# Trunk of two layers, float32: a weight sum of the MLP's seven-product scheme made by GpSimd instead of VectorE

## The chip, the cores and the metric

The program runs on 1 core of one Trainium2 chip. The metric is the device time of one execution in microseconds (us). The engines are TensorE (PE in the profile), VectorE (DVE), ScalarE (ACT), GpSimd (POOL) and SyncE (SP). The work of each engine is a queue in a fixed order; semaphores hold an instruction until its inputs are there.

## What is computed

The input `x` is 256 rows of 2048 numbers. Layer 1 is attention with forget gates, then an MLP; layer 2 is attention over chunks with a shared K/V, then an MLP. All weights are float32. The change lies in the two MLPs and in the query projection of layer 2, each a large matrix product:

```python
def sq_relu_mlp(h, g, w1, w2):            # w1: 2048 x 8192, w2: 8192 x 2048
    a = jax.nn.relu(rms_norm(h, g) @ w1)
    return (a * a) @ w2
...
q = rms_norm((u @ b_w_q[l]).reshape(B, S, H, Dh), b_q_g[l])   # b_w_q: 2048 x 2048
```

## The kernel before

**Splitting.** Each float32 product is made of three TensorE passes. Weights arrive in tiles of 128 x 1024. For each, ScalarE rounds it into `hi` (line 292), VectorE makes `lo = weight - hi` (line 293), and TensorE multiplies activations by `hi`, the activations' low part by `hi`, and the activations by `lo` (lines 592, 594, 596). Three pairs of `hi` and `lo` exist, so that the splits can run at most about two tiles ahead of TensorE.

**Seven products in place of eight.** In the MLPs and the query projection, half of the depth is done by blocks: a 2 x 2 block product takes seven products, with sums of weight blocks as operands. The class `Pair` holds one such set. Its seven weight operands are called f0 to f6, in two halves s = 0, 1 of 128 x 1024 each, and they come from four weight blocks 11, 12, 21, 22:

```python
FORMS = ("11", "T3", "T2", "T1", "21", "T4", "22")
```

T3 is 12 + 22, added in memory by a DMA that GpSimd issues (`add_on`, line 324); T2 is T3 + 11, added by an engine into a tile of its own, `wT2` (`make`, line 331); T1 is 11 + 12, again such a DMA, onto the tile of 11 once f0 has been split and T2 has been made; T4 is T2 + 21, added by VectorE in place (line 322). `bring` (line 311) loads 11 and 12 by SP. The profile cuts the numbers from names: `wT` is `wT2`, and `w` is `w11` or `w12`.

**Pairs.** There are 34: for each MLP, four chunks with two pairs of the up-projection (`w10`, `w11`) and two of the down-projection (`w20`, `w21`), and two pairs (`q0`, `q1`) of the query projection. With two halves that makes 68 additions at line 331. The table `ORDER` writes the order of each kind of pair out by hand; `f` is a seven-product operand, `a` and `b` are plain weight tiles of the same pair, `r` those left over from the pair before:

```python
"w10": "f0 f1 r f2 r r f4 f3 r r f5 a f6 a a a b b",
"w11": "f0 r f1 r f2 f4 a r f3 r a a f5 a f6 b b",
"w20": "r f0 r r f1 f2 f4 f3 f5 a r r a r b f6 b",
"w21": "f0 f1 f2 r f3 f4 r a f5 r r f6 r b a r",
```

**Where T2 is made.** `issue` splits an operand, and `behind` then runs what the table `BEHIND` lists for it. `(0, 1, "make", 0)` stands at f0, so that `make` comes right behind the split of f0 of the same half. It reads the tiles of T3 and of 11 and writes `wT2`, whose last readers were the splits of f5 (T4) of the pair before.

**Other work.** GpSimd issues the accumulating DMAs of line 324, half of the small DMAs that turn activations (`moves`, line 456), and a few powers of 128 x 4 (line 691). VectorE also makes the activations' low parts (lines 421, 965), transposes (441), sums of activations (399 to 402), and the corrections of the seven products (637, 639). `keep_order` fixes the written order on VectorE, ScalarE, TensorE and SyncE; on GpSimd the scheduler sets it.

Of the kernel before, what the change touches and what calls it, by code (L numbers as in the profile page):

```python
# [12 lines left out]
ALU = mybir.AluOpType  # L13
# [85 lines left out]
def trunk(ctx: ExitStack, tc: tile.TileContext, t):  # L99
# [3 lines left out]
    V, S, G, TE, SY = nc.vector, nc.scalar, nc.gpsimd, nc.tensor, nc.sync  # L103
# [200 lines left out]
    def half(s):  # L304
        return slice(s * UN, (s + 1) * UN)
# [20 lines left out]
    def make(p, s):  # L326
        assert (not p.prev or p.prev.did(5)) and {("T3", s), ("11", s)} <= p.done
        p.done.add(("T2", s))
        if not s:
            p.t["T2"] = qkv.tile([P, BIG], F32, name="wT2", tag="Z", bufs=1)  # L330
        V.tensor_tensor(p.t["T2"][:, half(s)], p.t["T3"][:, half(s)], p.t["11"][:, half(s)], op=ALU.add)  # L331

    later = deque()

    def behind(p, i, s):
        for k in range(s, 2 if s == p.subs - 1 else s + 1):
            for d, own, f, *a in BEHIND.get((i, k), ()):
                q = p if own else p.next
                if q is not None and a[-1] < q.subs:
                    while len(later) < d + 1:  # L340
                        later.append([])
                    later[d].append(lambda f=f, q=q, a=a: WAYS[f](q, *a))

    WAYS = {"make": make, "add": add_on, "bring": bring}

    def fetch(ahead=AHEAD, early=EARLY):
# [82 lines left out]
    def steps(make):  # L429
        box = []  # L430

        def step():
            if not box:
                box.append(make())
            next(box[0])
        return step
# [706 lines left out]
```

## Time and profile before

| | before |
|---|---|
| median of 2 runs | 2119.57 us (2119.49 to 2119.66) |
| the profiled execution | 2115.48 us, its span 2113.7 us |
| TensorE busy | 2074.7 us, 98% of the span |
| VectorE busy | 1736.8 us, 82% |
| ScalarE busy | 1301.9 us, 62% |
| GpSimd busy | 354.1 us, 17% |
| granted TensorE clock | 0.998 |

The span runs from the first to the last instruction; the execution's own time is 1.8 us longer. A row of a group gives the source line, the engine, what is written from what, the shape and count, and then busy time and the mean of one in ns; behind the second bar it gives the idle time of the engine just before these instructions. A row of the timeline gives start and length in us, then the instruction, and in square brackets the idle time before it and what ended it; "x2" is two such instructions that follow each other, and their length is that of both.

### The profile page before, as it was taken

The page shows a single profiled execution, that of the slowest core. Times are in us where ns is not written, and L with a number is a line of the kernel's source. Part 1 is how long each engine was busy: PE and PEld are TensorE (multiplying, and loading weights), DVE is VectorE, ACT ScalarE, POOL GpSimd, SP SyncE. Part 2 cuts the span into 40 slices and gives each one's busy share as a digit, 9 for nine tenths or more (in the row PEclk, how much of TensorE's full clock was granted, in tenths as well). Part 3 has the DMA queues.
Part 4 walks back from the last instruction along what each step waited for, and adds up shares of the span by engine and source line. Part 5 has one row for each costly group of instructions (what it writes and reads, how often), then busy time and mean ns, then how long its engine had stood idle before and what let it go on. Part 6 is the DMA issues. An engine that isn't in the chain of part 4 may idle for free.

```text
span 2113.7 us, 27078 instructions
## 1 busy us (share of the span) xinstructions
PE 2074.7 (98%) x9114; PEld 1695.1 (80%) x9114; DVE 1736.8 (82%) x2003; ACT 1301.9 (62%) x1567; POOL 354.1 (17%) x552
## 2 busy tenths in 40 slices
PE   9999999999999999999999999999999999999999
PEld 7888888787887887887777888887878878878877
DVE  6777776998889889878989577768988998898897
ACT  6544445676567567557767445456765765675674
POOL 1101002221031022022224000022200310220220
PEclk9999999999999999999999999999999999999999
DMA  8777788889888888898786777888897898888884
GB/s 302 241 257 222 240 253 266 251 257 283 273 256 245 277 267 244 262 278 268 239 241 218 256 235 241 239 265 251 268 278 256 259 259 279 268 250 256 280 262 157
DMA packets 160636, 538.89 MB, mean 255 GB/s; under 512 B 42849, under 2 KB 68081, under 8 KB 125681
## 3 DMA queue, kind: packets, MB, share of 16 engines
q1 hardware_dynamic: 129136, 453.78, 61.3%
q0 software_dynamic: 31360, 83.39, 20.8%
q8 instruction: 71, 1.16, 0.2%
q14 instruction: 69, 0.56, 0.1%
HBM read 497.20 MB, written 15.75 MB: 243 GB/s over the span
## 4 chain that ended last, share of the span: by engine, by line
PE 83%; DMA 6%; DVE 6%; issue 3%; ACT 2%; SPq 0%; POOL 0%; ACTq 0%; DVEq 0%; POOLq 0%
PE acc L592 18%; PE acc L594 18%; PE acc L596 18%; PE po L592 5%; PE po L596 5%; PE po L594 5%; PE s L596 4%; PE s L592 4%; PE s L594 4%; DVE lo L293 3%; DMA raw<-in_s2a 2%; DMA q<-z 2%; ACT hi L292 2%; DVE wT L322 1%; DMA raw<-in_s2b 1%
## 5 line engine op out<-in xcount | busy, mean ns | idle before, releaser
L293 DVE TENSOR_TENSOR lo<-raw,hi 128x1024 fp32r<-128x1024 f32 (+1 forms) x634 | 759.5, 1214 | 221.2 <-ACT hi L292 208.9
L292 ACT ACTIVATE hi<-raw 128x1024 fp32r<-128x1024 f32 (+1 forms) x634 | 660.4, 1054 | 386.7 <-PE acc L594 224.5
L592 PE MATMUL acc<-hi,act 128*128 128x512 f32 x1644 | 459.0, 394 | 9.9 <-DVE acc L637 4.4
L596 PE MATMUL acc<-lo,act 128*128 128x512 f32 x1644 | 449.1, 390 | 0.3 <-DVE lo L293 0.3
L594 PE MATMUL acc<-hi,act 128*128 128x512 f32 x1644 | 449.1, 390 | 0.0
L592 PEld LDWEIGHTS acc<-hi,act 128*128 128x128 f32 x1644 | 306.1, 188 | 79.5 <-DVE acc L637 7.9
L596 PEld LDWEIGHTS acc<-lo,act 128*128 128x128 f32 x1644 | 307.5, 188 | 66.8 <-DVE lo L293 2.4
L594 PEld LDWEIGHTS acc<-hi,act 128*128 128x128 f32 x1644 | 308.5, 188 | 65.5 <-DVE act L387 0.5
L292 ACT ACTIVATE hi<-w 128x1024 fp32r<-128x1024 f32 x204 | 215.1, 1056 | 100.6 <-PE acc L594 39.6
L293 DVE TENSOR_TENSOR lo<-w,hi 128x1024 fp32r<-128x1024 f32 x204 | 244.5, 1216 | 27.9 <-ACT hi L292 27.2
L456 POOL DMA_DIRECT2D q<-z x336 | 174.1, 608 | 464.1 <-DVE z L441 253.8
L292 ACT ACTIVATE hi<-wT 128x1024 fp32r<-128x1024 f32 x136 | 142.4, 1057 | 65.7 <-PE acc L594 27.0
L293 DVE TENSOR_TENSOR lo<-wT,hi 128x1024 fp32r<-128x1024 f32 x136 | 162.7, 1218 | 21.9 <-ACT hi L292 21.8
L596 PE MATMUL s<-lo,act 128*128 128x512 f32 x476 | 137.7, 394 | 2.6 <-DVE lo L293 2.4
L592 PE MATMUL s<-hi,act 128*128 128x512 f32 x476 | 136.4, 391 | 0.8 <-ACT hi L292 0.8
L594 PE MATMUL s<-hi,act 128*128 128x512 f32 x476 | 135.5, 389 | 0.0
L596 PEld LDWEIGHTS s<-lo,act 128*128 128x128 f32 x476 | 87.9, 188 | 27.0 <-DVE lo L293 9.7
L592 PEld LDWEIGHTS s<-hi,act 128*128 128x128 f32 x476 | 89.4, 188 | 20.6 <-ACT hi L292 2.0
L594 PEld LDWEIGHTS s<-hi,act 128*128 128x128 f32 x476 | 89.5, 188 | 18.8
L691 POOL TENSOR_TENSOR rn<-vv,mhalf 128x4 f32<-128x4 f32 x32 | 44.3, 1398 | 336.4 <-DVE vv L690 336.3
L331 DVE TENSOR_TENSOR wT<-w,w 128x1024 f32<-128x1024 f32 x68 | 82.7, 1217 | 0.0
L322 DVE TENSOR_TENSOR wT<-wT,raw 128x1024 f32<-128x1024 f32 x68 | 82.7, 1216 | 0.0
(183 smaller groups left out, 2282.1 us busy)
## 6 DMA issues: line engine op xcount, KB each, us to landing
raw<-in_w_in SPq DMA_DIRECT2D x94, 512.0 KB, 5.5
raw<-in_s1a SPq DMA_DIRECT2D x32, 1024.0 KB, 6.4
raw<-in_s2a SPq DMA_DIRECT2D x32, 1024.0 KB, 6.9
raw<-in_w_kv SPq DMA_DIRECT2D x64, 512.0 KB, 5.5
raw<-in_s1b SPq DMA_DIRECT2D x32, 1024.0 KB, 7.0
raw<-in_s2b SPq DMA_DIRECT2D x32, 1024.0 KB, 6.7
raw<-in_w_oa SPq DMA_DIRECT2D x32, 512.0 KB, 6.3
w<-in_f1a SPq DMA_DIRECT2D x16, 1024.0 KB, 7.0
```

Of the source, the lines that this page charges most:

```text
L292: S.activation(hi[:, c], raw[:, c], AF.Copy)
L293: V.tensor_tensor(lo[:, c], raw[:, c], hi[:, c].bitcast(F32), op=ALU.subtract)
L322: V.tensor_tensor(d, d, p.t["21", s], op=ALU.add)
L331: V.tensor_tensor(p.t["T2"][:, half(s)], p.t["T3"][:, half(s)], p.t["11"][:, half(s)], op=ALU.add)
L456: (SY, G)[j % 2].dma_start(d[32 * j : 32 * j + 32, i], z[32 * i : 32 * i + 32, j * n : (j + 1) * n])
L592: TE.matmul(ps, xh, cut(hi, j), start=first, stop=False, **kw)
L594: TE.matmul(ps, xl, cut(hi, j), start=False, stop=False, **kw)
L596: TE.matmul(ps, xh, cut(lo, j), start=False, stop=last, **kw)
L691: G.tensor_tensor(rn, vv, mhalf, op=ALU.pow)
```

## The change

The addition of T2 is issued on GpSimd's queue (`G` is `nc.gpsimd`, `V` is `nc.vector`). The place in the source is the same.

```diff
     def make(p, s):
         assert (not p.prev or p.prev.did(5)) and {("T3", s), ("11", s)} <= p.done
         p.done.add(("T2", s))
         if not s:
             p.t["T2"] = qkv.tile([P, BIG], F32, name="wT2", tag="Z", bufs=1)
-        V.tensor_tensor(p.t["T2"][:, half(s)], p.t["T3"][:, half(s)], p.t["11"][:, half(s)], op=ALU.add)
+        G.tensor_tensor(p.t["T2"][:, half(s)], p.t["T3"][:, half(s)], p.t["11"][:, half(s)], op=ALU.add)
```

On GpSimd, at the first `w20` and `w21` pair of layer 1 (`w11_3995` and `w11_4328` are their tiles of 11, `q` rows are the turning DMAs, `in_f2a0` and `in_f2a1` the weights), the queue now reads, with + for rows that are new:

```order
 L324 DMA w12_3808<-in_f2a0 128x1024 x2
 L456 DMA q_3836<-z_3835 32x256 x8
+L331 TENSOR_TENSOR wT2_4096<-w12_3808,w11_3995 128x1024 x2
 L456 DMA q_4034<-z_4033 32x256 x8
 L324 DMA w11_3995<-in_f2a0 128x1024 x2
 L456 DMA q_4187<-z_4186 32x256 x8
 L324 DMA w12_4204<-in_f2a1 128x1024 x2
+L331 TENSOR_TENSOR wT2_4394<-w12_4204,w11_4328 128x1024 x2
 L324 DMA w11_4328<-in_f2a1 128x1024 x2
```

Both additions of a pair stand together, ahead of the DMAs that make T1, and at the `w20` pair ahead of eight turning DMAs too. On VectorE, at the same `w21` pair, the two rows are gone and the splits close up:

```order
 L293 TENSOR_TENSOR lo_4381<-raw_4220,hi_4380 128x1024
 L293 TENSOR_TENSOR lo_4391<-w11_4328,hi_4390 128x1024
-L331 TENSOR_TENSOR wT2_4394<-w12_4204,w11_4328 128x1024
 L293 TENSOR_TENSOR lo_4404<-w11_4328,hi_4403 128x1024
-L331 TENSOR_TENSOR wT2_4394<-w12_4204,w11_4328 128x1024
 L293 TENSOR_TENSOR lo_4421<-w12_4204,hi_4420 128x1024
 L293 TENSOR_TENSOR lo_4436<-w12_4204,hi_4435 128x1024
```

The addition on GpSimd is no longer tied to VectorE's place behind f0: it may start when T3 and 11 are there and `wT2` is free. The order on TensorE, ScalarE and SyncE is unchanged.

## The prediction
> **What bounds the kernel now.** I read the page first, then TensorE's waits. Section 1 of the page:
>
> ```profile
> span 2113.7 us, 27078 instructions
> PE 2074.7 (98%) x9114; PEld 1695.1 (80%) x9114; DVE 1736.8 (82%) x2003; ACT 1301.9 (62%) x1567; POOL 354.1 (17%) x552
> ```
>
> TensorE leaves 39 us of the whole span. What it waited for, from the table of waits (total, times, longest):
>
> ```profile
> PE po L592 <- DVE s L637: 12.7, 9, 3.9
> PE acc L592 <- DVE acc L637: 4.4, 8, 0.6
> PE s L596 <- DVE lo L293: 2.4, 8, 0.8
> PE acc L596 <- DVE lo L293: 0.7, 2, 0.4
> ```
>
> So a lighter VectorE can give back 12.7 + 4.4 + 2.4 + 0.7 = 20 us at most, 1% of the time. TensorE is the bound, and the question is whether the change makes it wait for `lo` more often than now. Around 2% is what a measurement of this kernel can tell from no change.
>
> **What is removed, and what is added.** The group of the additions, and what GpSimd has of like kind (groups by form, and its powers alone, where the three numbers are min, median and max in ns):
>
> ```profile
> L331 DVE TENSOR_TENSOR wT<-w,w 128x1024 f32<-128x1024 f32 x68 | 82.7, 1217 | 0.0
> L865 POOL MEMSET act<- 128x2048 f32 x1 | 1.8, 1794 | 0.0
> L529 POOL TENSOR_TENSOR rx<-msx,mhalf 128x2 f32<-128x2 f32 x1 | 0.7, 717 | 39.9 <-DVE msx L549 39.9
> L691 POOL TENSOR_TENSOR rn<-vv,mhalf x32: 1003/1417/1905, 47.8 to 1320.3; 128x4 f32<-128x4 f32 x32
> ```
>
> VectorE loses 68 x 1.217 = 82.7 us of work. No row shows GpSimd adding two tiles of 1024. Its memset writes one stream of 2048 in 1.794 us, 0.88 ns an element. Below, two input streams one behind the other are 2 x 1024 x 0.88 = 1.8 us; with the 0.72 us of its smallest operation on top they are 2.5; above, three streams and 0.72 are 3.4 us. I take S = 2.3, nearer to the middle value than to the bare streams because the small operations show that the fixed part is real. The Trainium skill, GPSIMD Engine Reference, section 3.1, gives 4497 ns for a two-input add of 2048, so an estimate of 2.25 us for this one; by it the sum below would be 3 us smaller.
>
> **Do the two engines keep each other out?** Two powers on GpSimd, and VectorE at the same time:
>
> ```profile
> 1131.78 1.03 POOL L691 TENSOR_TENSOR rn<-vv,mhalf 128x4 f32<-128x4 f32 x1 [2.26 <-DVE vv L690]
> 1135.28 1.91 POOL L691 TENSOR_TENSOR rn<-vv,mhalf 128x4 f32<-128x4 f32 x1 [2.47 <-DVE vv L690]
> 1131.92 1.23 DVE L421 TENSOR_TENSOR act<-y,act 128x1024 fp32r<-128x1024 f32 x1 [0.29 <-ACT act L420]
> 1135.09 1.23 DVE L293 TENSOR_TENSOR lo<-raw,hi 128x1024 fp32r<-128x1024 f32 x1
> ```
>
> The first power started with no two-input operation of VectorE in flight and took 1.03 us, though one began 0.14 us later. The second started while `lo` ran, and ended at 1137.19, 0.87 us after that `lo` ended at 1136.32. So GpSimd stood until VectorE's operation with two inputs in on-chip memory was over. The other direction is not shown: four elements hold nothing up that can be seen. Its bounds are nothing, and the whole length S of each addition. I take the whole, since the direction that is seen is a full wait and not a slowing. The Trainium skill, SBUF — State Buffer, section "Who interferes with whom", says the same of both directions: a VectorE operation with two inputs in SBUF and a GpSimd operation that reads it exclude each other for the whole instruction. By that rule the whole sum below stands; the rows above agree for the one direction.
>
> Then VectorE gives away 1.217 us an addition and is shut for up to 2.3, a net loss for an engine that has hardly a pause where this falls. How much TensorE sees is read kind by kind: late = time shut - work that needs no shutting and idle time of VectorE - T2 slots already saved - how long `lo` was ready before its use.
>
> **w20** (8 pairs; first one). SP's load of 11, as the timeline and the DMA table (KB, us to landing) of that moment have it, then VectorE, its idle time, and TensorE's use of `lo`:
>
> ```profile
> 448.04 0.33 SPq L311 DMA_DIRECT2D w<-in_f2a  x1
> w<-in_f2a SPq DMA_DIRECT2D x1, 1024.0 KB, 6.7
> 454.46 1.22 DVE L293 TENSOR_TENSOR lo<-raw,hi 128x1024 fp32r<-128x1024 f32 x1
> 455.60 1.31 DVE L441 STREAM_TRANSPOSE z<-acc 128x512 f32<-128x512 f32 x2
> 456.83 2.31 DVE L293 TENSOR_TENSOR lo<-raw,hi 128x1024 fp32r<-128x1024 f32 x2
> 462.91 1.22 DVE L331 TENSOR_TENSOR wT<-w,w 128x1024 f32<-128x1024 f32 x1
> 464.04 0.42 DVE L399 TENSOR_TENSOR sum<-q 128x256 f32<-128x256 f32 x1
> 467.24 1.23 DVE L293 TENSOR_TENSOR lo<-w,hi 128x1024 fp32r<-128x1024 f32 x1 [0.26 <-ACT hi L292]
> 454.80:467.24 12.44, 11.77 (x16) 1.00 0.84 292
> 468.52 0.73 PE L596 MATMUL s<-lo,act 128*128 128x512 f32 x2
> ```
>
> 11 lands at 448.04 + 6.7 = 454.8, eight us ahead of VectorE's old slot at 462.91, and GpSimd starts then. It waits for the `lo` in flight until 455.68, runs under the transposes (which read PSUM), and holds the next `lo`, due at 456.83, for S - 1.15. The second addition holds VectorE for S. By 467.24 VectorE makes up its idle time, 12.44 - 11.77 = 0.67, and one saved slot, 464.04 - 462.91 = 1.13. That `lo` ends at 468.47 and is used at 468.52, 0.05 us later. Late: 2S - 1.15 - 0.67 - 1.13 - 0.05 = 2S - 3.0 = 1.6 us, times 8 = 12.8.
>
> **w21** (8 pairs; first one):
>
> ```profile
> 483.91 0.33 SPq L311 DMA_DIRECT2D w<-in_f2a  x1
> w<-in_f2a SPq DMA_DIRECT2D x1, 1024.0 KB, 11.6
> 495.84 2.36 DVE L293 TENSOR_TENSOR lo<-raw,hi 128x1024 fp32r<-128x1024 f32 x2 [0.48 <-ACT hi L292]
> 500.41 1.07 PE L596 MATMUL po<-lo,act 128*128 128x512 f32 x4
> ```
>
> 11 lands at 495.5; VectorE idles until 495.84, so the first addition holds it for S - 0.34. If GpSimd takes its second turn right after one `lo`, the second `lo`, which ended at 498.20 for a use at 500.41 (2.21 early), is late by 2S - 0.34 - 2.21 = 2.05. Both T2 slots come after. Not every pair starts with so little in hand, so I count 1.8 x 8 = 14.4.
>
> **w10, w11, q.** The second w10 pair, and the idle time of VectorE at the first w11 pair:
>
> ```profile
> 531.66 0.74 DVE L728 SCALAR_TENSOR_TENSOR h<-po,qm,h 128x512 f32<-128x512 f32 x1
> 533.97 2.36 DVE L293 TENSOR_TENSOR lo<-raw,hi 128x1024 fp32r<-128x1024 f32 x2 [1.56 <-ACT hi L292]
> 535.95 1.08 PE L596 MATMUL acc<-lo,act 128*128 128x512 f32 x4
> 408.50:414.21 5.71, 4.56 (x5) 1.00 0.66 273
> ```
>
> Before 533.97 VectorE idles 1.56 us behind an operation on PSUM, so one addition is hidden and the second reaches some 1 us into a `lo` that was 535.95 - 535.20 = 0.75 early: 0.3 us late. At w11 1.15 of 5.71 us are idle; I put 0.3 there too. That makes 16 x 0.3 = 4.8, and q0 and q1, which start like w20, 2 us.
>
> **The sum.** 12.8 + 14.4 + 4.8 + 2 = 34 us. The profiled execution takes 2115.48 us, 1.8 more than its span, and would take 2149.5; the median of the runs is 4.1 above it. Forecast: 2119.57 + 34 = 2154 us, 1.6% slower. With S = 1.8 the terms are 0.6, 0.8 and nothing, some 13 us; with 2.5 they are 2.0, 2.2 and 0.5, and 45 with q; with 3.4 (late by 3.8, 4.0 and 2 us, q 6) 100 us.
>
> I cost at nothing that T2 itself comes from a slower engine: in these two kinds it starts 8.1 and 3.8 us before its old slot. Without that head start both additions would end 2S - 2.4 = 2.2 us later than now, and f2's split with them. T1's DMAs wait for the split of f0 anyway.
>
> **The rivals.**
>
> *No shutting out: faster.* If GpSimd reads beside VectorE without holding it, VectorE drops 2.43 us a pair, which exceeds each of the nine waits on `s L637` but one (3.9 at longest). Some 12.7 + 2.4 = 15 us go: 2105 us. For it speaks that no VectorE row shows a wait for GpSimd's reading; against it the power that stood for the `lo`. It decides if additions hold VectorE by under 1.2 us each. Chance 0.2.
>
> *A dearer addition.* From S = 2.5 the loss passes 2%; at 3.4 it is 100 us, 2220. For it: powers of four elements take 1 us. Against it: reading and writing would have to go one after the other. Typical of this case is S = 2.8, some 60 us, 2180. Chance 0.3.
>
> *GpSimd's queue.* At w20 eight turning DMAs now stand behind both additions:
>
> ```profile
> 457.44 3.90 POOL L456 DMA_DIRECT2D q<-z  x8 [13.29 <-ACT hi L292]
> q<-z POOLq DMA_DIRECT2D x8, 32.0 KB, 6.1
> 470.84 1.06 ACT L954 ACTIVATE q<-q 128x1024 f32<-128x1024 f32 x1
> ```
>
> They land some 6.1 us after their issue, up to 467.4; ScalarE needs them at 470.84, and all splits queue behind that instruction. The additions, 454.8 to about 461.5 with one wait, push the issue back by 4 us, past the 3.4 in hand. If they land still later, by 2 us, 8 pairs cost 16 more: 2170 us. Chance 0.1.
>
> **How the numbers follow.** Forecast 0.4, no shutting 0.2, a dearer addition 0.3, the queue 0.1. The range goes from 2104, just past the first rival, to 2220, the dearest addition. Slower by over 2% (above 2162): nearly all of the dearer addition, half of the queue, a twelfth of the forecast, 0.38. Faster by over 2% needs 42 us where TensorE has 39 idle: 0.02. Within 2%: 0.60.
>
> **What would show it.** Right: TensorE's order unchanged, its waits on `lo L293` and on `s L637` up from 20 to some 50 us, most in w20 and w21; `lo` rows with two inputs longer than 1.23 us at the side of an L331 row on POOL, or pauses there; additions of 2 to 3.5 us with their waits, several us before the old slot. Wrong: `lo` at 1217 ns throughout and fewer waits on L637 (no shutting out); ScalarE waiting at L954 (the queue); L331 rows of over 3 us with nothing to wait for (dearer).

## The result, and the profile after

The changed kernel takes 2179.41 us (median of 2 runs, 2178.01 to 2180.82), against 2119.57 before: 1.028 times as long, with a 95% interval from 1.024 to 1.033. The profiled execution takes 2180.82 us, and its span is 65.0 us longer than that of before. From section 1 of the page after:

```profile
span 2178.7 us, 27081 instructions
PE 2097.2 (96%) x9114; PEld 1696.1 (78%) x9114; DVE 1774.8 (81%) x1935; ACT 1302.9 (60%) x1567; POOL 553.1 (25%) x620
```

VectorE lost 68 instructions and is busy 38 us *longer*. TensorE does the same 9114 matmuls; its idle time went from 39.0 to 81.5 us, and its busy time grew by 22.5. The additions and the splits by source line (minimum, median and maximum in ns, then the first and last start):

```profile
L331 POOL TENSOR_TENSOR wT<-w,w x68: 2369/3111/3474, 369.6 to 2114.4; 128x1024 f32<-128x1024 f32 x68
L293 DVE TENSOR_TENSOR lo<-raw,hi x634: 691/1220/3466, 6.0 to 2166.6; 128x1024 fp32r<-128x1024 f32 x158, 128x512 fp32r<-128x512 f32 x1
L293 DVE TENSOR_TENSOR lo<-w,hi x204: 1180/1217/5417, 370.0 to 2146.8; 128x1024 fp32r<-128x1024 f32 x102
L293 DVE TENSOR_TENSOR lo<-wT,hi x136: 1207/1218/1227, 387.5 to 2144.5; 128x1024 fp32r<-128x1024 f32 x136
```

An addition alone takes 2.37 us; the longer ones stood first until VectorE's two-input operation was over. A split that met one addition has a record of up to 3.47 us in place of 1.22: it was shut out for 2.25 us. Two splits of `w`, at the first w10 pair of each layer, stood through both additions of their pair and have records of 5.42 and 5.15 us. The splits of T2 and T4 themselves (`wT`) keep their length; no addition runs beside one of them. What TensorE waited for now:

```profile
PE po L596 <- DVE lo L293: 15.9, 14, 1.7
PE po L592 <- DVE s L637: 13.9, 9, 5.1
PE s L596 <- DVE lo L293: 9.9, 14, 2.1
PE po L592 <- ACT hi L292: 9.3, 11, 2.4
PE s L592 <- ACT hi L292: 6.4, 7, 1.3
PE acc L596 <- DVE lo L293: 6.2, 13, 0.8
PE acc L592 <- DVE acc L637: 4.4, 8, 0.6
PE acc L592 <- ACT hi L292: 2.1, 4, 0.7
```

Waits for `lo` went from 3.1 to 32.0 us, those for the corrections L637 from 17.1 to 18.3, and those for ScalarE's `hi` from 7.5 to 17.8. The first w20 and w21 pairs, as four rows of before and then nine of after:

```profile
464.95 1.30 ACT L405 ACTIVATE Sh<-sum 128x512 fp32r<-128x512 f32 x2 [3.60 <-DVE sum L400]
490.96 1.06 ACT L954 ACTIVATE q<-q 128x1024 f32<-128x1024 f32 x1 [4.03 <-DMA w<-in_f2a]
493.02 1.19 PE L592 MATMUL po<-hi,act 128*128 128x512 f32 x4
494.97 1.07 PE L596 MATMUL po<-lo,act 128*128 128x512 f32 x4
```

```profile
461.44 6.48 POOL L331 TENSOR_TENSOR wT<-w,w 128x1024 f32<-128x1024 f32 x2 [11.73 <-DMA w<-in_f2a]
463.45 5.55 DVE L293 TENSOR_TENSOR lo<-raw,hi 128x1024 fp32r<-128x1024 f32 x2
473.24 1.30 ACT L405 ACTIVATE Sh<-sum 128x512 fp32r<-128x512 f32 x2 [5.27 <-DVE sum L400]
475.54 0.73 PE L592 MATMUL s<-hi,act 128*128 128x512 f32 x2 [1.20 <-ACT hi L292]
500.86 1.06 ACT L954 ACTIVATE q<-q 128x1024 f32<-128x1024 f32 x1 [4.92 <-DMA q<-z]
502.78 5.73 POOL L331 TENSOR_TENSOR wT<-w,w 128x1024 f32<-128x1024 f32 x2 [12.93 <-DMA w<-in_f2a]
502.90 8.97 DVE L293 TENSOR_TENSOR lo<-raw,hi 128x1024 fp32r<-128x1024 f32 x4 [3.72 <-ACT hi L292]
502.92 1.19 PE L592 MATMUL po<-hi,act 128*128 128x512 f32 x4 [0.82 <-ACT hi L292]
506.31 1.19 PE L596 MATMUL po<-lo,act 128*128 128x512 f32 x4 [1.28 <-DVE lo L293]
```

**w20.** The two splits behind the transposes take 5.55 us in place of the 2.31 before. VectorE reaches its four sums late, ScalarE stands at L405 for 5.27 us instead of 3.60, and the rounding queued behind L405 is what TensorE waits for. Later in the pair ScalarE stands at L954 for a turned `q`.

**w21.** The additions start at 502.78, 0.12 us before a split whose `lo` has no slack. Between the two matmul rows lie 494.97 - 493.02 = 1.95 us before and 506.31 - 502.92 = 3.39 after: 1.44 us lost there. The second addition stretches the next split in the same way.

**The clock.** At the first w11 pair TensorE waits twice, and a stretch at a lower granted clock follows (rows by stretch: PE busy, clock, DMA share, GB/s):

```profile
414.17 1.19 PE L594 MATMUL s<-hi,act 128*128 128x512 f32 x4 [0.75 <-DVE act L421]
417.48 1.19 PE L596 MATMUL s<-lo,act 128*128 128x512 f32 x4 [2.12 <-DVE lo L293]
410.00:420.00 10.00, 6.88 (x26) 0.94 0.49 187
420.00:430.00 10.00, 10.00 (x41) 0.89 0.67 213
```

The loss of clock in the two rows, 0.6 + 1.1 = 1.7 us, is one spell of 3.4 us at half clock. Before has 6.8 us of such spells ahead of its last instructions, after 20.5. So some 6.8 us of TensorE's added busy time is half clock. The other 15.7 I read as the price of a wait beyond the wait itself: at 506.31 the row shows 1.28 us idle where 1.44 were lost. Compared matmul by matmul with before, at the some 40 places where a wait grew and no spell is near, TensorE lost 52 us where its idle time grew by 40. Why a stop costs more than its wait was not tested.

The account of the 65.0 us: waits on `lo` and L637, 30.1; waits on ScalarE's `hi`, 10.3; other waits, 2.1; half clock, 6.8; the rest of the longer busy time, 15.7.

### The profile page after: what moved, and what is told of

It reads as the page before. It is cut to its first block, busy times and chain, and to the rows that moved or that the text cites. A ratio compares the mean times of both kernels' runs of the same rounds, so it can differ in the third digit from the quotient of the medians.

```text
span 2178.7 us, 27081 instructions
## 1 busy us (share of the span) xinstructions
PE 2097.2 (96%) x9114; PEld 1696.1 (78%) x9114; DVE 1774.8 (81%) x1935; ACT 1302.9 (60%) x1567; POOL 553.1 (25%) x620
## 3 DMA queue, kind: packets, MB, share of 16 engines
q0 software_dynamic: 31360, 83.39, 20.2%
## 4 chain that ended last, share of the span: by engine, by line
PE 69%; DMA 12%; DVE 10%; issue 4%; ACT 3%; SPq 1%; ACTq 0%; POOL 0%; DVEq 0%; POOLq 0%
PE acc L596 16%; PE acc L594 16%; PE acc L592 16%; DVE lo L293 7%; PE po L596 4%; PE po L592 4%; PE po L594 3%; DMA q<-z 3%; PE s L596 3%; PE s L594 3%; PE s L592 3%; ACT hi L292 3%; DMA raw<-in_s2a 2%; DMA raw<-in_s2b 2%; DMA raw<-in_s1b 1%
## 5 line engine op out<-in xcount | busy, mean ns | idle before, releaser
L293 DVE TENSOR_TENSOR lo<-raw,hi 128x1024 fp32r<-128x1024 f32 (+1 forms) x634 | 856.1, 1368 | 213.6 <-ACT hi L292 207.0
L293 DVE TENSOR_TENSOR lo<-w,hi 128x1024 fp32r<-128x1024 f32 x204 | 255.2, 1267 | 48.9 <-ACT hi L292 46.3
L331 POOL TENSOR_TENSOR wT<-w,w 128x1024 f32<-128x1024 f32 x68 | 198.9, 2941 | 377.7 <-DMA w<-in_f1b 90.1
L596 PE MATMUL s<-lo,act 128*128 128x512 f32 x476 | 138.9, 396 | 10.3 <-DVE lo L293 9.9
L596 PEld LDWEIGHTS s<-lo,act 128*128 128x128 f32 x476 | 88.1, 189 | 37.4 <-DVE lo L293 20.2
```

The source lines that it names most:

```text
L293: V.tensor_tensor(lo[:, c], raw[:, c], hi[:, c].bitcast(F32), op=ALU.subtract)
L331: G.tensor_tensor(p.t["T2"][:, half(s)], p.t["T3"][:, half(s)], p.t["11"][:, half(s)], op=ALU.add)
L596: TE.matmul(ps, xh, cut(lo, j), start=False, stop=last, **kw)
```

## The experiments

The first four ran beside one median of before and the next four beside another; both are 2117.61 us. The theory: while GpSimd reads for an addition, VectorE's two-input operations stand, and the change costs what TensorE sees of that. Where an edit adds a line, the numbers of the lines behind it are one higher.

### The parts of the change: e1, e2, e3

GpSimd makes the sum only in w20 pairs, only in w21 pairs, or only in the others:

```diff
-        G.tensor_tensor(p.t["T2"][:, half(s)], ...)
+        E = G if (p.stage[0], p.n) == ("w2", 0) else V      # e1
+        E = G if (p.stage[0], p.n) == ("w2", 1) else V      # e2
+        E = G if p.stage[0] != "w2" else V                  # e3
+        E.tensor_tensor(p.t["T2"][:, half(s)], ...)
```

> GpSimd adds T2 in the 8 w20 pairs alone, VectorE in the other 26. Theory (each addition shuts VectorE's two-input operations out for about 2.3 us, and what TensorE sees depends on how far ahead the splits are): the trace of the change shows 1.5 us lost before f0 of a w20 pair, some 0.5 behind it and 1.0 at the Relu that waits for the turning DMAs; 8 x 3.0 = 24 us, near 2144. The prediction's own term was 12.8 us, 2132. Rival (VectorE is freed, nothing shut out): 2105 to 2110.

> GpSimd adds T2 in the 8 w21 pairs alone. Theory: two stalls of 1.5 us a pair, one for each addition, 8 x 3.0 = 24 us, near 2144, and no ScalarE wait that was not there before. The prediction's term was 14.4 us, 2134. Rival (the loss comes from the turning DMAs behind the additions): no such DMA stands behind these, so 2120.

> GpSimd adds T2 in w10, w11, q0 and q1 alone, 18 pairs. Theory: the loss sits in the first w10 and the first w11 pair of each layer (1.4 to 2.1 and 5.0 us in the trace of the change, part of it at half the granted clock) and in q0 and q1 (3 us); about 17 us, 2137, and next to nothing in the other 12. The prediction's terms were 4.8 + 2 = 7 us, 2126. If the three kinds add up, the three losses make the 60 us of the change.

| | pairs | predicted term | measured | ratio and interval |
|---|---|---|---|---|
| e1 | 8 w20 | 12.8 us | 2145.19, +27.6 | 1.0129 (1.0110 to 1.0149) |
| e2 | 8 w21 | 14.4 us | 2145.62, +28.0 | 1.0132 (1.0116 to 1.0148) |
| e3 | 16 w10 and w11, q0, q1 | 6.8 us | 2133.60, +16.0 | 1.0084 (1.0066 to 1.0102) |

The split over the kinds is as the prediction had it, in the same order for the first two, and each term is about twice its size. The row of TensorE's waits that grew most, first e1, then e2, then e3:

```profile
PE po L593 <- ACT hi L292: 13.2, 12, 2.7
```

```profile
PE po L597 <- DVE lo L293: 11.7, 14, 1.7
```

```profile
PE s L597 <- DVE lo L293: 9.2, 12, 2.1
```

In e1 the loss reaches TensorE mostly through ScalarE. Its rows at the first w20 pair:

```profile
467.46 1.31 ACT L406 ACTIVATE Sh<-sum 128x512 fp32r<-128x512 f32 x2 [5.27 <-DVE sum L401]
473.52 1.06 ACT L955 ACTIVATE q<-q 128x1024 f32<-128x1024 f32 x1 [0.17 <-DMA q<-z]
495.40 1.06 ACT L955 ACTIVATE q<-q 128x1024 f32<-128x1024 f32 x1 [5.82 <-DMA q<-z]
```

The delay at the sums costs TensorE 1.45 us there, close to the 1.6 that the prediction has for a w20 pair. Then the later of the two waits for a turned `q` grows from 4.03 to 5.82 us and costs another 1.8. At the earlier one, which the prediction's queue rival named, ScalarE hardly waits (0.17). In e3, matmul by matmul against before, the first w11 pair of layer 1 loses 5 us (3.4 of delay and a spell of half clock), that of layer 2 3.1, where 0.3 each was put, and the first q pair some 3, where 1 was.

The three parts add up to 71.6 us, and the whole change costs 61.8 against the same median of before. I did not follow where the 10 us overlap.

### Writing without reading: e4

```diff
-        G.tensor_tensor(p.t["T2"][:, half(s)], p.t["T3"][:, half(s)], p.t["11"][:, half(s)], op=ALU.add)
+        for _ in range(2):
+            G.memset(p.t["T2"][:, half(s)], 0.0)
```

> In place of each addition GpSimd writes zeros into the same half of wT2, twice (2 x 0.9 us by the memset row of before): the sum T2 is left out. GpSimd is about as long busy as with the addition, and VectorE is as much lighter, but GpSimd reads nothing. Theory (it is the reading that VectorE and GpSimd exclude each other from): no stretched splits, VectorE's saved 82.7 us come through where TensorE waited for it, 2100 to 2110. Rival (GpSimd's time or its queue costs, whatever it does): as the change, 2165 to 2180. If writing alone excludes too: the splits are stretched by 0.9 us, 2125 to 2150.

2122.94 us, ratio 1.0022 (1.0008 to 1.0037). By source line, and one of the waits:

```profile
L332 POOL MEMSET wT<- x136: 942/955/1647, 309.4 to 2053.1; 128x1024 f32 x136
L293 DVE TENSOR_TENSOR lo<-raw,hi x634: 691/1224/1229, 6.0 to 2109.9; 128x1024 fp32r<-128x1024 f32 x158, 128x512 fp32r<-128x512 f32 x1
PE po L593 <- DVE s L638: 14.1, 9, 5.3
PE po L593 <- ACT hi L292: 12.4, 10, 2.2
```

The time is above the 2100 to 2110 that were expected. GpSimd is in use for 1.9 us a half here, and no split is longer than 1.23 us. Two things follow. A GpSimd instruction that only writes does not shut VectorE out. And a VectorE that is 69.8 us lighter and never shut out gains *nothing*: the waits on the correction (L637 before) stay. The rival "no shutting out: faster" was wrong in its price, 15 us.

A third thing bears on e1. TensorE's waits on ScalarE's `hi` grew here too, from 7.5 to 16.4 us, and most of them follow a wait of ScalarE for a turned `q` at L954 (L955 here). At the first w20 pair that wait is 5.97 us and TensorE's 1.84, close to e1's 5.82 and 1.72. Matmul by matmul against before, the stretch of the later L954 in the eight w20 pairs costs 11.0 us in e1 and 9.4 in e4 (in before's time, from 10 us behind ScalarE's last wait at L405 to 4.5 us behind its later stop at L954). So this part of w20's loss does not need VectorE to be shut out. What differs at the first w20 pair is how long the last two turning DMAs take from SP's issue to landing: 7.6 and 8.1 us in before, 9.9 and 10.4 in e4, 9.8 and 10.2 in e1. In e4 and e1 both accumulating DMAs of the next pair's T3 (line 324) are issued ahead of the two, in before the second of them comes between the two. Whether that is the reason was not tested.

### More and less of it: e6, e7, e8

One stream read instead of two; each addition as two of 512 columns; each addition made twice:

```diff
+        G.tensor_copy(p.t["T2"][:, half(s)], p.t["T3"][:, half(s)])          # e6, in place of the addition
+        for c in (slice(s * UN, s * UN + 512), slice(s * UN + 512, (s + 1) * UN)):   # e7
+            G.tensor_tensor(p.t["T2"][:, c], p.t["T3"][:, c], p.t["11"][:, c], op=ALU.add)
+        for _ in range(2):                                                   # e8
+            G.tensor_tensor(p.t["T2"][:, half(s)], ...)
```

> GpSimd copies T3 into the tile of T2 and does not read 11, so the values of T2 lack 11. One stream is read instead of two. Theory (what shuts VectorE out is the reading, for as long as it lasts): a shorter instruction, some 1 to 1.3 us, shuts VectorE out for about what it saved, 2115 to 2130 us. Rival (each instruction of GpSimd that reads holds VectorE by the same 2.2 us whatever it reads): 2165 to 2180 us with L293 rows of up to 3.4 us.

> Each addition on GpSimd is made as two of 512 columns, so that VectorE can take turns between them. Theory (the sum of the time shut out counts, since the splits of these places are late as a whole): 2165 to 2185 us, with twice as many stretched L293 rows, each stretched by half (up to 2.4 us). Rival (the length of one hold counts, because a single split is what TensorE waits for): some 2150 us.

> Each addition on GpSimd is made twice over with the same result. Theory: another 2.25 us shut per addition. Where the first already makes TensorE late (w20 and w21, 16 pairs), both count in full or nearly: 16 x 4.2 = 67 us; in the other 18 pairs, where part is hidden, about 2 us each, 36; in all 2250 to 2290 us. Rival (the loss comes from where the addition starts or from a fixed part, not from its length): 2180 to 2200 us.

GpSimd's instructions and the splits, for e6, e7 and e8 in turn:

```profile
L331 POOL COPY wT<-w x68: 1037/1174/2383, 318.1 to 2063.7; 128x1024 f32<-128x1024 f32 x68
L293 DVE TENSOR_TENSOR lo<-raw,hi x634: 693/1220/2066, 6.2 to 2118.4; 128x1024 fp32r<-128x1024 f32 x158, 128x512 fp32r<-128x512 f32 x1
```

```profile
L332 POOL TENSOR_TENSOR wT<-w,w x136: 1264/2269/2380, 369.3 to 2111.5; 128x512 f32<-128x512 f32 x136
L293 DVE TENSOR_TENSOR lo<-raw,hi x634: 691/1224/2332, 6.5 to 2156.7; 128x1024 fp32r<-128x1024 f32 x158, 128x512 fp32r<-128x512 f32 x1
```

```profile
L332 POOL TENSOR_TENSOR wT<-w,w x136: 2334/3372/3485, 369.4 to 2234.1; 128x1024 f32<-128x1024 f32 x136
L293 DVE TENSOR_TENSOR lo<-raw,hi x634: 684/1224/3449, 6.3 to 2281.8; 128x1024 fp32r<-128x1024 f32 x158, 128x512 fp32r<-128x512 f32 x1
```

With e4 as the level without shutting out, since VectorE has the same 1935 instructions in all of them:

| | one instruction shuts out for | VectorE busy above e4 | time (above before) | ratio and interval |
|---|---|---|---|---|
| e4, writes only | 0 | 0 | 2122.94 (+5) | 1.0022 (1.0008 to 1.0037) |
| e6, one stream | 0.85 us | 26 us | 2134.76 (+17) | 1.0081 (1.0054 to 1.0109) |
| e7, two halves | 2 x 1.11 us | 105 us | 2170.94 (+53) | 1.0262 (1.0229 to 1.0295) |
| after | 2.25 us | 108 us | 2179.41 (+62) | 1.0282 (1.0238 to 1.0327) |
| e8, twice | 2 x 2.23 us | 255 us | 2296.59 (+179) | 1.0854 (1.0823 to 1.0885) |

The second column is the longest `lo<-raw` split less 1.22 us. (One split of `w`, at the first w10 pair, stands through all additions of its pair; its record is 10.0 us in e8, which has four.) The time rises with what VectorE is shut out, not with the number of instructions, so the theory stands, and e7 says that it is the sum that counts and not the length of one hold. e6 came out 5 us above its expected range. Its hold of 0.85 us is shorter than the slot of 1.13 that VectorE saves, and still it costs. A copy that does not read 11 starts earlier than an addition: at the w20 pairs it falls on the four sums, two of which take 1.15 and 1.26 us there in place of 0.42. ScalarE waits for them at L405, and TensorE for ScalarE, 1.08 us in each of the eight pairs, which is most of this row:

```profile
PE acc L592 <- ACT hi L292: 12.0, 13, 1.1
```

Compared matmul by matmul, these eight places cost 11 us. So e6 and e4 differ from after in the place as well as in the hold.

e8 lies 7 us above its range; its granted clock was 0.984, against 0.995 after, which is some 25 us of the 115 that its span is longer.

### GpSimd in the written order: e5

```diff
-    keep_order(tc, (V.engine, S.engine, TE.engine, SY.engine))
+    keep_order(tc, (V.engine, S.engine, TE.engine, SY.engine, G.engine))
```

> The additions stay on GpSimd, but its queue keeps the written order, so that at w20 six of the eight turning DMAs are issued ahead of the additions. Theory (VectorE is shut out while GpSimd reads, by some 2.2 us an addition; the queue is a small part): ScalarE's waits at L954 for the turned q go back from 47 to some 25 us, the stretched splits stay, time 2165 to 2175 us. Rival (most of w20's loss is that the additions hold up the turning DMAs): some 2150 us, as e1's 27 us would then mostly go.

2189.77 us, ratio 1.0345 (1.0317 to 1.0373): outside both expectations. ScalarE's waits in all, and the first w20 pair:

```profile
ACT Sh L405 <- DVE sum L400: 74.6, 16, 6.9
ACT q L954 <- DMA q<-z: 7.3, 4, 2.1
468.86 2.98 POOL L456 DMA_DIRECT2D q<-z  x6 [14.14 <-ACT hi L292]
471.85 5.87 POOL L331 TENSOR_TENSOR wT<-w,w 128x1024 f32<-128x1024 f32 x2
479.62 1.30 ACT L405 ACTIVATE Sh<-sum 128x512 fp32r<-128x512 f32 x2 [6.87 <-DVE sum L400]
481.92 1.22 PE L592 MATMUL s<-hi,act 128*128 128x512 f32 x2 [2.34 <-ACT hi L292]
```

The waits at L954, with those that the profile puts down to other DMAs, went from 46.9 to 19.5 us, further than expected, and nothing was gained. With the turning DMAs ahead of them the additions fall on the two splits right before the four sums, so that ScalarE waits 6.87 us at L405 instead of 5.27. TensorE's wait of 2.34 us there returns in seven w20 pairs, each with a spell of half clock beside it. Matmul by matmul, the stretch of the later L954 costs 21 us less in the eight pairs than in after, and the stretch of the sums ahead of it 19 more; the rest of the rise lies in other pairs. At the first w10 pair of layer 1 TensorE loses 5.3 us where it lost 1.7 in after. So the order of GpSimd's queue does act on the waits at L954, but a fixed order also moves the additions, and e5 does not show the one without the other.

### VectorE's order instead of its load: e9

All sums stay on VectorE; the second addition of T4 moves behind the split of f4's second half, so that the corrections no longer queue behind it:

```diff
-    (4, 1): [(0, 1, "add", "T4", 1), (8, 0, "add", "T3", 1)],
+    (4, 1): [(1, 1, "add", "T4", 1), (8, 0, "add", "T3", 1)],
```

> All additions of T2 on VectorE as before. In the table BEHIND the second half's addition of T4 goes from behind f4's first split to behind its second, so that the corrections L637 and L639 no longer queue behind it. Theory (the waits of TensorE on s L637, 12.7 us in 9 places, are set by VectorE's order and not by its load): they shrink by 1.1 us each, some 9 us in all, 2110 us, a ratio of 0.996. Rival (the waiting only moves to the splits behind): 2120 us, with waits on lo L293 in place of those on L637.

2147.56 us, ratio 1.014 (1.0112 to 1.0168) against a median of before of 2116.20. Two of TensorE's waits, then ScalarE and TensorE at the first w20 pair, and the clock of that stretch:

```profile
PE po L592 <- ACT hi L292: 22.3, 9, 3.6
PE po L592 <- DVE s L637: 4.5, 1, 4.5
482.02 1.06 ACT L292 ACTIVATE hi<-wT 128x1024 fp32r<-128x1024 f32 x1 [1.83 <-DVE wT L322]
492.42 1.06 ACT L954 ACTIVATE q<-q 128x1024 f32<-128x1024 f32 x1 [6.49 <-DMA q<-z]
494.47 1.40 PE L592 MATMUL po<-hi,act 128*128 128x512 f32 x4 [2.33 <-ACT hi L292]
490.00:500.00 10.00, 7.67 (x27) 0.83 0.62 240
```

The theory is right in its first half: the waits on L637 shrink by 8.2 us (and the 4.4 of `acc` are gone) through order alone, with VectorE's load unchanged. But the second addition of T4 comes 1.7 us later behind the first, and ScalarE waits for it. The addition also frees the weight tile that SP's next load needs: that load is issued at 481.98 in place of 481.08, and two turning DMAs that stand behind it on SP at 482.36 in place of 481.82; they take 9.4 and 9.0 us to land, in place of 7.6 and 8.1. ScalarE stands 6.49 us at L954, TensorE 2.33, and half a clock for 3.4 us follows: 14 us more idle time and 18 more of busy time over the span. The rival had the waiting move on at no cost and for another engine; it moved on at a price of 31 us. No version here beats before.

## Why the prediction came out as it did

**Right: the bound, the mechanism and the direction.** VectorE gave up 1.2 us and was shut out for up to 2.25 an addition (1.6 on average, from the 108 us above e4), where S = 2.3 was taken; an addition alone took 2.37 (2.25 was the estimate from the Trainium skill, GPSIMD Engine Reference, section 3.1). The direction that no row of before showed, GpSimd holding VectorE, is a full wait, as assumed. The Trainium skill, SBUF — State Buffer, section "Who interferes with whom", says that a VectorE operation with two inputs there contends with a GpSimd instruction that reads, and not with one that only writes; after and e4 agree with both halves. The waits on `lo` and L637 were to go from 20 to some 50 us; they went from 20.2 to 50.3.

**The step that failed: "late" was taken for the whole loss.** The sum's 34 us are close to the 30.1 us of added waits on `lo` and L637. Its formula asked when a `lo` comes too late at TensorE and stopped there. Beside it stand 10.3 us of waits on ScalarE's `hi`, 6.8 of half clock and 15.7 of longer busy time, none of which the sum had. Not all of the 10.3 stands behind a late VectorE: e4 has 8.9 more than before without any shutting out. The measured time lies inside the range that was given, but the range was drawn that wide for a dearer addition, which did not come.

**Term by term.** *w20*, 12.8 for 27.6: the direct 1.6 us is there (1.45 at e1's first pair, up to 3 at others, 18 us in all eight), though it passes through the sums and L405 and not through the `lo` at 467.24. The rest is the later L954, 11 us, where the sum counted no delay; as e4 shows, that is mostly not the shutting out. *w21*, 14.4 for 28.0: the slack of 0.34 + 2.21 us was counted on, but in after the tile of 11 arrived 0.12 us before an earlier split without slack, and both additions were seen, at 1.4 to 1.5 us each. *The others*, 6.8 for 16.0: in after the first w11 pair of each layer lost 5 us instead of 0.3. There VectorE's L421 is shut out first, then the first split, and half clock follows.

**The rivals.** *A dearer addition* gave 2180 us, the measured time, by a cause that did not happen: that price needs S = 2.8, and the additions hold for 2.25. *GpSimd's queue* was counted as turning DMAs held up behind the additions at the earlier L954. There ScalarE hardly waits; the later one grew (34.1 us of waits at L954 in before, 46.9 in after). The written order removes that in e5, though the additions then fell on a worse place, and e4 has it without an addition: a part of the loss, some 9 us if after has it as e4 does, is not VectorE shut out but transfers that land later, by a path that the rival did not name. *No shutting out* is denied by the stretched splits, and e4 denies its gain as well: the waits on L637 hang on VectorE's order (e9), so that 20 us of "possible gain" were not to be had from a lighter VectorE.

## What to carry to other kernels

In these runs an operation moved from VectorE to GpSimd cost VectorE the time that GpSimd read, wherever VectorE was running operations with two on-chip inputs; compare that hold, and not GpSimd's idle time, with the slot saved. When a bound engine is delayed, do not stop at its first wait: price the engine that queues behind the same late operand, the restart, and the clock as well. A change of one queue also moves transfers in time, and what that costs shows only in a kernel without the effect under study, as e4 is here. And a wait is a gain to be had only if what it waits for would really come earlier; a kernel that leaves the work out tells that at once.

## What was not expected of the hardware

**Half clock after waits of 2 us.** Nearly every wait of TensorE of 2.1 us or more has a spell of 3.4 or 6.8 us at half the granted clock beside it, in before (one, at 1073 us, beside a wait of 3.9), in after and in e5, e8 and e9; single waits of up to 1.9 us mostly have none, and a few longer ones have none either. Every run has a wait of about 1 us and 2.4 us behind it one of 1.66 at the same matmuls; seven of the eleven traces have a spell there, after among them (1186.84) and before not, so that one of after's spells may be chance. The starts of the spells lie a whole number of 3.413 us apart (418.84 and 1026.41 in after: 178 times). The Trainium skill, TensorE: Matmul & The Clock Gate, Part 1, has a free-running window of 3413 ns and a fall to half clock after an idle one. The spacing agrees; here a wait of 2.12 us that fills only part of such a window was enough. At 1.7 us a spell, this is a small part of the change's loss, and some 14 of the 31 us of e9.

**What shuts VectorE out is short of GpSimd's whole time.** A copy of 1.04 us holds it for 0.85, an addition of 2.37 for 2.25, one of 512 columns of 1.26 for 1.11, and writes of 0.95 not at all.
